# A streaming encoder on one NeuronCore: the merging gates of the first 768 tokens computed as paired products in the projection phase

## The chip, the cores and the metric

The kernel runs on 1 core of one Trainium2 chip. The metric is the device time of one execution in microseconds (us); lower is better. A NeuronCore has a matrix engine (TensorE, PE in the profile, with its weight loads shown as PEld), three engines for elementwise work (VectorE = DVE, ScalarE = ACT, GpSimd = POOL), and SyncE (SP), whose queue issues the DMA transfers here. The engines run side by side, each in its own program order, and wait for each other by semaphores.

## What is computed

One layer with two attention branches. T is 2048 prompt tokens and 128 new tokens of eight running streams, 2176 in all; the model width is 1024. Cut to what matters:

```python
h = rms_norm(x, g_in)
proj = einsum('btd,de->bte', h, w_in)
qa, ka, va, z_a, qd, ckv_in, kpe_in, z_b, m_a, m_b = split(proj)
o_a = diff_attention(...)            # 4 heads, two softmaxes each
o_b = mla_attention(...)             # 4 heads on a compressed latent
y_a = einsum('btw,wd->btd', rms_norm(o_a) * silu(z_a), w_oa)
y_b = einsum('btw,wd->btd', o_b * silu(z_b), w_ob)
merged = sigmoid(m_a) * y_a + sigmoid(m_b) * y_b     # m_a, m_b: the merging gates
out = x + einsum('btd,de->bte', merged, w_out)
```

The merging gates m_a and m_b are 2 x 1024 columns of the input projection: 16 units of 128 columns. The kernel stores tanh(m/2) for each, in `c.smT`, and the last phase makes the sigmoid out of it. All of it is float32; a matmul of full accuracy is made of three float32r matmuls (high x high, low x high, high x low parts of the operands).

## The kernel before

Work runs in five phases, one after the other on the whole: A, the input projections; A2, the second projections of the latent branch (Qn, Qp, Kn, Vb); B, the attention of the prompt; S, the attention of the streams; C, the output projections.

**Phase A** (`_phase_a`, L125) goes over three parts of the tokens (`PARTS`, L38: 768, 768 and 640 tokens, each cut in two halves of n = 384, 384 and 320 columns). A part first loads and normalises its tokens, makes the V block and the rotary key block, and then runs 11 *pairs* (`pairs`, L396). A pair (`pair_products`, L326) computes two units of 128 output columns for both halves at once, by Strassen's scheme in Winograd's form: seven products of 12 matmuls each, 84 matmuls of n columns, where the plain form needs 96. Its weights (`pair_weights`, L292) are two loads of 512 KB, four sums on DVE (L304, kept for later parts by a store of 1 MB to `c.wsum`, L305) and seven splits into high and low parts (`_split`, ACT L114 and DVE L115); its outputs are put together by one ACT copy and seven DVE additions (L335). The weight tiles have eleven buffers in two pools, so they are made ahead of the matmuls.

**The merging gates** are not in phase A. `_gates` (L423) computes them for one group of tokens (`GROUPS`, L36: five groups of 384 and a sixth of 256), 16 units of 24 matmuls each into a single PSUM bank (pool `z_p`, tile `z`), followed by a tanh on ACT (L464) that frees the bank, and a store to `c.smT`. A unit's weights are either loaded as they are (512 KB) and split, or, with `ready`, loaded already split from the scratch `c.wz` (two loads of 512 KB); group 1 stores its split weights there (two stores of 512 KB a unit, L458). Weight tiles `zw` have four buffers, two units.

**What sets the order.** The kernel is written against a framework that orders each engine's instructions by a simulated timeline with priorities. Loads and evacuation of `_gates` get the priority of the point behind phase A (`ahead`), their matmuls that of the place where `_gates` is called, behind phase B. So the gate matmuls are *filler*: the scheduler places them on PE wherever its timeline has PE idle in A2 and B. The order that it makes is fixed in the program; on the chip each engine keeps it. Groups 0, 1, 2 and 5 are called ahead of `_sample` (L1377) and fill A2 and B; groups 3 and 4 fill phase S. In the order of before, A2 holds the 384 matmuls of group 0, and phase B the 1152 of groups 1, 2 and 5.

**Phase B** (`_phase_b`, L1006) runs 4 heads x 8 blocks of 256 queries, 32 steps, each a block of the differential branch (its blocks upwards) and one of the latent branch (downwards): scores on PE, row maximum on DVE (L1077), exponential on ACT (L1079), scaling on POOL and DVE, transposes on PE, splits on ACT and DVE, products with the values on PE.

Of the kernel before, what the change touches and what calls it, by code (L numbers as in the profile page):

```python
# [14 lines left out]
AF = mybir.ActivationFunctionType  # L15
# [24 lines left out]
PARTS = [(0, 384), (768, 384), (1536, 320)]  # L40
# [72 lines left out]
def _split(nc, hi, lo, src):  # L113
    nc.scalar.copy(hi, src)  # L114
    nc.vector.tensor_tensor(lo, src, hi.bitcast(F32), op=ALU.subtract)  # L115
# [13 lines left out]
def _phase_a(c):  # L129

    nc, tc = c.nc, c.tc
    with (
# [14 lines left out]
        def stage(shape, name):  # L147
            return turn("st", 2, pst, c.zs).tile(shape, F32, tag="st", name=name)

        def operand(shape, name):  # L150
            return turn("w", 3, pw, c.zw).tile(shape, F32R, tag="w", name=name)
# [140 lines left out]
        def pair_weights(p, u, nm):  # L292
            st = [stage([P, KT, P], f"ws_{nm}_{i}") for i in range(2)]
            nc.sync.dma_start(st[0], c.i["wu"][u])
            sums = pq.tile([P, 4, 4, P], F32, tag="s", name=f"s_{nm}")
            a11, a12 = (st[0][:, k : k + 4] for k in (0, 4))
            s1, s2, s3, s4 = (sums[:, i] for i in range(4))
            if p == 0:
                nc.sync.dma_start(st[1], c.i["wu"][u + 1])
                a21, a22 = (st[1][:, k : k + 4] for k in (0, 4))  # L300
                for out, x, y, op in (
                    (s1, a21, a22, ALU.add), (s2, s1, a11, ALU.subtract), (s4, a12, s2, ALU.subtract), (s3, a11, a21, ALU.subtract)
                ):
                    nc.vector.tensor_tensor(out, x, y, op=op)  # L304
                nc.sync.dma_start(c.wsum[u // 2], sums)  # L305
            else:

                a22 = st[1][:, 4:8]
                nc.sync.dma_start(sums, c.wsum[u // 2])
                nc.sync.dma_start(a22, c.i["wu"][u + 1][:, 4:8])  # L310
            ops = []
            for i, x in enumerate((a11, a12, s4, a22, s2, s3, s1)):
                w = operand([P, KT, P], f"w{i}_{nm}")
                _split(nc, w[:, 0:4], w[:, 4:8], x)
                ops.append(w)
            return ops
# [37 lines left out]
        def rope_pair(p, u, dst, pair, out, scale):  # L354
            t0, n = PARTS[p]
            res = pair_products(p, u, f"r{u}_{p}")
            for half in range(2):
                nm = f"r{u}_{p}_{half}"
                cols = slice(t0 + half * n, t0 + half * n + n)
                cs = pc.tile([P, 2, NG], F32, tag="cs", name=f"cs{nm}", bufs=2)[:, :, :n]  # L360
                nc.sync.dma_start(cs, c.i["rope"][:, :, cols])
                co, si = cs[:, 0], cs[:, 1]
                ta, tb = res[0][half], res[1][half]
                m1, m2, m3, m4 = (tmp(n, f"m{i}{nm}") for i in range(4))
                nc.vector.tensor_tensor(m1, ta, co, op=ALU.mult)
                nc.vector.tensor_tensor(m2, tb, si, op=ALU.mult)
                nc.vector.tensor_tensor(m3, tb, co, op=ALU.mult)
                nc.vector.tensor_tensor(m4, ta, si, op=ALU.mult)
                nc.vector.tensor_tensor(m1, m1, m2, op=ALU.subtract)
                nc.vector.tensor_tensor(m3, m3, m4, op=ALU.add)  # L370
                for a, (r, x, y) in enumerate(((m1, ta, m2), (m3, tb, m4))):
                    if out is not None:
                        nc.sync.dma_start(out[pair, a, :, cols], r)
                    xr, yr = x.bitcast(F32R), y.bitcast(F32R)
                    nc.scalar.mul(xr, r, scale)
                    nc.vector.scalar_tensor_tensor(yr, r, scale, x, op0=ALU.mult, op1=ALU.subtract)
                    for hl, z in enumerate((x, y)):
                        nc.sync.dma_start(dst[pair, hl, a, :, cols], z)
# [8 lines left out]
        def gate_pair(p, u, out):  # L387
            t0, n = PARTS[p]
            res = pair_products(p, u, f"g{u}_{p}")
            for i in range(2):  # L390
                for half in range(2):
                    z = res[i][half]
                    nc.scalar.activation(z, z, AF.Silu)
                    nc.sync.dma_start(out[i][:, t0 + half * n : t0 + half * n + n], z)

        def pairs(p):  # L396
            rope = [lambda a=a: rope_pair(p, 2 * a, c.Qs, a, None, DIFF_SCALE) for a in range(2)]
            rope += [lambda a=a: rope_pair(p, 4 + 2 * a, c.Ks, a, c.o["kT"], 1.0) for a in range(2)]
            lat = [lambda a=a: latent_pair(p, 8 + 2 * a, [c.qdT[2 * a], c.qdT[2 * a + 1]]) for a in range(2)]
            lat.append(lambda: latent_pair(p, 12, [c.ckT[0], c.ckT[1]]))  # L400
            gate = [lambda a=a: gate_pair(p, 14 + 2 * a, [c.gzT[2 * a], c.gzT[2 * a + 1]]) for a in range(4)]
            mixed = [f for z in zip(rope, gate) for f in z]
            return [lat[0], *mixed, lat[1], lat[2]]

        for t in range(2 * PARTS[0][1] // P):
# [17 lines left out]
def _gates(c, prio, g, after, ready):  # L423

    nc, tc = c.nc, c.tc

    def ahead():
        return tc.high_priority(offset=tc.cur_priority - prio)

    t0, n = GROUPS[g]  # L430
    with ahead():
        R = c.zh.tile([P, NG], F32, tag="R", name=f"Rz{g}")[:, :n]
        nc.sync.dma_start(R, c.Rh[:, t0 : t0 + n])
        hi = c.zh.tile([P, KT, NG], F32R, tag="hi0", name=f"z_hi{g}")[:, :, :n]
        lo = c.zh.tile([P, KT, NG], F32R, tag="lo0", name=f"z_lo{g}")[:, :, :n]
        for k2 in range(4):
            x = c.zs.tile([P, 2, NG], F32, tag="st", name=f"zx{g}_{k2}")[:, :, :n]
            nc.sync.dma_start(x, c.i["xT"][:, 2 * k2 : 2 * k2 + 2, t0 : t0 + n])
            for j in range(2):
                k = 2 * k2 + j  # L440
                nc.vector.scalar_tensor_tensor(x[:, j], x[:, j], c.g_in[:, k : k + 1], R, op0=ALU.mult, op1=ALU.mult)
                nc.scalar.copy(hi[:, k], x[:, j])
                nc.vector.tensor_tensor(lo[:, k], x[:, j], hi[:, k].bitcast(F32), op=ALU.subtract)
    for u in range(16):
        nm = f"{g}_{u}"
        with ahead():
            w = [c.zw.tile([P, KT, P], F32R, tag="w", name=f"zw{l}_{nm}") for l in range(2)]
            if ready:
                for l in range(2):
                    nc.sync.dma_start(w[l].bitcast(F32), c.wz[u, l])  # L450
            else:
                st = c.zs.tile([P, KT, P], F32, tag="st", name=f"zs{nm}")
                nc.sync.dma_start(st, c.i["wu"][22 + u])
                for k in range(0, KT, 4):
                    _split(nc, w[0][:, k : k + 4], w[1][:, k : k + 4], st[:, k : k + 4])
                if g == 1:
                    for l in range(2):
                        nc.sync.dma_start(c.wz[u, l], w[l].bitcast(F32))  # L458
        ps = c.zp.tile([P, 512], F32, tag="z", name=f"z{nm}")[:, :n]
        with tc.issue_after(after) if after else nullcontext():  # L460
            _mm3(nc, ps, [(w[0][:, k], w[1][:, k], hi[:, k], lo[:, k]) for k in range(KT)])
        with ahead():
            s = c.zt.tile([P, NG], F32, tag="t", name=f"zt{nm}")[:, :n]
            nc.scalar.activation(s, ps, AF.Tanh, scale=0.5)  # L464
            nc.sync.dma_start(c.smT[u][:, t0 : t0 + n], s)
# [898 lines left out]
def build(tc, ins, outs, upto="z", dump=None):  # L1364
    c = Ctx()
    c.tc, c.nc = tc, tc.nc
    c.i, c.o = ins, outs
    with tc.tile_pool(name="const", bufs=1) as pool, tc.tile_pool(name="dram", bufs=1, space=DRAM) as dpool:
        _consts(c, pool)
        _scratch(c, dpool)  # L1370
        with ExitStack() as stack:
            _outer(c, stack)
            _phase_a(c)
            prio = tc.cur_priority
            _phase_a2(c)
            _phase_b(c)
            for g in (0, 1, 2, 5):  # L1377
                _gates(c, prio, g, None, g in (2, 5))
            _sample(c, stack)
            for g in (3, 4):  # L1380
                _gates(c, prio, g, c.mm.ins, False)
        _phase_c(c)
        for name, cut in (dump or {}).items():
            c.nc.sync.dma_start(c.o["d_" + name], cut(getattr(c, name)))
# [92 lines left out]
```

## Time and profile before

| | us |
|---|---|
| median of 3 runs | 2594.69 (2593.53 to 2594.82) |
| the profiled execution | 2595.66 |
| its span, first to last instruction | 2593.9 |
| PE busy | 2418.1 (93%) |
| DVE busy | 1645.4 (63%) |
| ACT busy | 1224.7 (47%) |
| POOL busy | 470.4 (18%) |
| DMA queue 1 moved | 550.46 MB, 64.0% of the time of 16 engines |

The shares are averages over phases with different limits, so they are to be read by phase: A ends at 621 us (its last pair matmul), A2 at 874 us, phase B at 1778, S at 2187. "PE busy" counts matmuls from start to modelled end, and matmuls overlap; the number of matmuls in a stretch is the firmer measure. PEclk is the share of full TensorE clock that was granted. "DMA" is the mean busy share of the core's 16 DMA engines.

### The profile page before, as it was taken

What the parts mean: (1) busy time and instruction counts of PE and PEld (TensorE: products, weight loads), DVE (VectorE), ACT (ScalarE), POOL (GpSimd) and SP (SyncE); (2) the same over time, 40 slices, a digit from 0 to 9 for tenths busy, and PEclk for the clock granted to TensorE, in tenths of its full rate; (3) what the DMA queues carried; (4) which work ended last, traced back from release to release, by engine and by line L of the source; (5) the groups of instructions that cost most, each with busy time, mean ns of one, the idle gap of its engine ahead of it and who ended that gap; (6) DMA issues with size and microseconds to landing.
All of it is one profiled execution on the core that took longest, in us unless ns stands there. A gap on an engine that the chain in (4) does not pass through costs nothing. (4 is left out here: it accounts for less than half of the span.)

```text
span 2593.9 us, 44001 instructions
## 1 busy us (share of the span) xinstructions
PE 2418.1 (93%) x15426; PEld 2149.4 (83%) x15426; DVE 1645.4 (63%) x3668; ACT 1224.7 (47%) x3042; POOL 470.4 (18%) x730
## 2 busy tenths in 40 slices
PE   6998999997899699999999988998999997999998
PEld 5998999997888689899888977887676674988887
DVE  7897686886676477877776688894333223534334
ACT  5544544543444366766665566783334333311111
POOL 0000000000000032333343234443000002122211
PEclk9999999999899899999999999999999998999999
DMA  6977677686687986574666755316869594544332
GB/s 236 306 268 251 210 252 265 204 280 185 228 277 255 299 285 201 183 227 140 182 194 207 232 170 166 92 58 232 325 254 370 222 380 138 174 128 126 121 115 96
DMA packets 303997, 553.28 MB, mean 213 GB/s; under 512 B 29184, under 2 KB 230176, under 8 KB 288544
## 3 DMA queue, kind: packets, MB, share of 16 engines
q1 hardware_dynamic: 303776, 550.46, 64.0%
q8 instruction: 123, 2.02, 0.3%
q14 instruction: 98, 0.80, 0.1%
HBM read 397.16 MB, written 153.19 MB: 212 GB/s over the span
## 5 line engine op out<-in xcount | busy, mean ns | idle before, releaser
L100 PE MATMUL z<-z_hi,zw 128*128 128x384 f32 (+1 forms) x768 | 264.7, 345 | 47.1 <-ACT zt L464 28.2
L102 PE MATMUL z<-z_hi,zw 128*128 128x384 f32 (+1 forms) x768 | 257.9, 336 | 0.4 <-DVE zw L115 0.4
L101 PE MATMUL z<-z_lo,zw 128*128 128x384 f32 (+1 forms) x768 | 258.1, 336 | 0.1
L1079 ACT ACTIVATE ed<-sd,pmd 128x512 f32<-128x512 f32 (+3 forms) x320 | 201.1, 632 | 43.6 <-DVE pmd L1077 23.0
L1077 DVE TENSOR_REDUCE pmd<-sd 128x1 f32<-128x512 f32 (+3 forms) x320 | 189.4, 603 | 49.9 <-PE sd L1178 30.6
L1178 PE MATMUL sd<-k,q 128*128 128x512 f32 (+2 forms) x640 | 193.1, 391 | 13.3 <-ACT ed L1079 8.9
L100 PEld LDWEIGHTS z<-z_hi,zw 128*128 128x128 f32 x768 | 148.6, 193 | 68.6 <-ACT zt L464 36.1
L1118 POOL TENSOR_SCALAR ed<-ed,ad 128x512 f32<-128x512 f32 (+3 forms) x160 | 115.5, 737 | 317.5 <-DVE ad L1094 142.5
L101 PEld LDWEIGHTS z<-z_lo,zw 128*128 128x128 f32 x768 | 148.8, 194 | 7.3 <-issue 4.1
L102 PEld LDWEIGHTS z<-z_hi,zw 128*128 128x128 f32 x768 | 147.9, 193 | 6.5 <-issue 3.4
L109 POOL TENSOR_SCALAR ss<-ss 128x3 f32<-128x3 f32 (+3 forms) x15 | 3.2, 213 | 792.4 <-DVE ss L529 474.1
L115 DVE TENSOR_TENSOR zw<-zs,zw 128x512 fp32r<-128x512 f32 x128 | 84.4, 688 | 92.9 <-ACT zw L114 90.8
L100 PE MATMUL y<-o,wh_ab 128*128 128x384 f32 (+1 forms) x384 | 127.8, 333 | 13.7 <-DVE sm L1303 10.5
L1118 POOL TENSOR_SCALAR em<-em,am 128x512 f32<-128x512 f32 (+3 forms) x160 | 102.9, 660 | 185.5 <-DVE am L1094 115.5
L101 PE MATMUL y<-o,wh_ab 128*128 128x384 f32 (+1 forms) x384 | 126.6, 330 | 0.0
L102 PE MATMUL y<-o,wl_ab 128*128 128x384 f32 (+1 forms) x384 | 126.3, 329 | 0.0
L1178 PEld LDWEIGHTS sd<-k,q 128*128 128x128 f32 x640 | 105.4, 194 | 23.6 <-ACT ed L1079 15.5
L1079 ACT ACTIVATE em<-sm,pmm 128x512 f32<-128x512 f32 (+3 forms) x160 | 100.2, 629 | 47.0 <-DVE pmm L1077 34.2
L1303 DVE SCALAR_TENSOR_TENSOR sm<-sm,y 128x384 f32<-128x384 f32 (+1 forms) x96 | 50.4, 530 | 112.9 <-PE y L102 111.4
L1308 ACT ACTIVATE m<-sm 128x384 fp32r<-128x384 f32 (+1 forms) x48 | 24.3, 506 | 199.0 <-POOL sm L1306 199.0
L1077 DVE TENSOR_REDUCE pmm<-sm 128x1 f32<-128x512 f32 (+3 forms) x160 | 95.6, 603 | 35.3 <-PE sm L1225 27.4
L1135 ACT CAST pthd<-ptd 128x512 fp32r<-128x512 f32 (+3 forms) x160 | 82.6, 522 | 72.1 <-PE ptd L1132 69.6
(521 smaller groups left out, 7579.3 us busy)
## 6 DMA issues: line engine op xcount, KB each, us to landing
zs<-in_wu_dram SPq DMA_DIRECT2D x64, 512.0 KB
zw<-wz SPq DMA_DIRECT2D x64, 512.0 KB
ksd<-in_ckT_dram SPq DMA_DIRECT2D x32, 1024.0 KB
vsd<-in_cv_dram SPq DMA_DIRECT2D x32, 1024.0 KB
q<-Qs SPq DMA_DIRECT2D x128, 128.0 KB
wz<-zw SPq DMA_DIRECT2D x32, 512.0 KB
ksm<-in_cc_dram SPq DMA_DIRECT2D x16, 1024.0 KB
smT<-zt SPq DMA_DIRECT2D x80, 192.0 KB
```

Source lines behind the costliest of these rows:

```text
L100: nc.tensor.matmul(out, ah, bh, start=(j == 0), stop=False)
L101: nc.tensor.matmul(out, ah, bl, start=False, stop=False)
L102: last = nc.tensor.matmul(out, al, bh, start=False, stop=(j == n - 1))
L109: c.nc.gpsimd.tensor_scalar(ss, ss, scale, EPS, op0=ALU.mult, op1=ALU.add)
L115: nc.vector.tensor_tensor(lo, src, hi.bitcast(F32), op=ALU.subtract)
L1077: nc.vector.tensor_reduce(nm_, ps[:, :w], axis=AX.X, op=ALU.max, negate=True)
L1079: nc.scalar.activation(e[:, :w], ps[:, :w], AF.Exp, bias=nm_, accum_out=l[:, s, i : i + 1])
L1118: nc.gpsimd.tensor_scalar(p, p, a[:, 0, j : j + 1], 1.0, op0=ALU.mult, op1=ALU.mult)
L1135: nc.scalar.copy(hi, v)
L1178: nc.tensor.matmul(ps[:, :n], qs[s][:, j, qc], ks[s].tiles[i][:, :n], start=(j == 0), stop=(j == 1 and not last))
L1303: nc.vector.scalar_tensor_tensor(s, s, 1.0, ps, op0=ALU.add, op1=ALU.mult)
L1308: nc.scalar.mul(z[0], sm[0], 0.5)
```

## The change

The 16 units of merging gates of the first 768 tokens (groups 0 and 1) move into phase A: part 0 gets eight more pairs (`merge_pair`), behind the rotary and gate pairs and ahead of the last two latent pairs. Each is a pair like the others, with tanh on its four outputs and four stores of 192 KB to `c.smT`; its weight sums are not kept for later parts, since only part 0 uses them. `_gates` is then called for groups 2 and 5 alone ahead of `_sample`; group 2 splits its weights itself and stores them in `c.wz`, as group 1 did, and group 5 loads them from there. Groups 3 and 4 stay as they are.

```diff
+                if u < 22:
+                    nc.sync.dma_start(c.wsum[u // 2], sums)
...
+        def merge_pair(p, u):
+
+            t0, n = PARTS[p]
+            res = pair_products(p, 22 + u, f"m{u}_{p}")
+            for i in range(2):
+                for half in range(2):
+                    z = res[i][half]
+                    nc.scalar.activation(z, z, AF.Tanh, scale=0.5)
+                    nc.sync.dma_start(c.smT[u + i][:, t0 + half * n : t0 + half * n + n], z)
...
+            if p == 0:
+                mixed += [lambda u=u: merge_pair(p, u) for u in range(0, 16, 2)]
             return [lat[0], *mixed, lat[1], lat[2]]
...
-                if g == 1:
+                if g == 2:
                     for l in range(2):
                         nc.sync.dma_start(c.wz[u, l], w[l].bitcast(F32))
...
-            for g in (0, 1, 2, 5):
-                _gates(c, prio, g, None, g in (2, 5))
+            for g in (2, 5):
+                _gates(c, prio, g, None, g == 5)
```

In the order that the scheduler makes, three places differ most. In the rows below a name like `zw0_5_7` is the tile `zw`, high part (0), of group 5, unit 7; the last number of a name counts tiles.

In part 0 of phase A, the SP queue behind the last store of the silu gates (`gzT`). Before:

```order
L394 DMA gzT_86<-u3g20_0_2002 128x384
L309 DMA s_r0_1_2991<-wsum_96 128x2048
L385 DMA qdT_83<-m1l10_0_2142 128x384
L279 DMA ws_kpe1_2797<-in_wkpe_dram 128x512
L385 DMA qdT_83<-wl10_0_2145 128x384
```

Now:

```order
L395 DMA gzT_86<-u3g20_0_2002 128x384
L294 DMA ws_m8_0_0_2675<-in_wu_dram 128x1024
L405 DMA smT_87<-m1m0_0_2141 128x384
L299 DMA ws_m8_0_1_2676<-in_wu_dram 128x1024
L405 DMA smT_87<-wm0_0_2144 128x384
L405 DMA smT_87<-vm0_0_2142 128x384
L405 DMA smT_87<-u3m0_0_2143 128x384
```

The latent pairs and the loads of part 1 stand eight pairs later; per pair there are two weight loads and four stores.

In A2, the SP queue at the stores of Qn of the third group of tokens. Before:

```order
L601 DMA Qn_88<-qnz2_1_7369 128x2x384
L601 DMA Qn_88<-qnz2_2_7386 128x2x384
L560 DMA out_ckT_dram<-ck3_7313 128x2x384
L601 DMA Qn_88<-qnz2_3_7403 128x2x384
L509 DMA qd4_7593<-qdT_83 128x4x384
L610 DMA cs3_7764<-in_rope_dram 128x2x384
L511 DMA ck4_7595<-ckT_84 128x2x384
L583 DMA kcs4_7866<-in_ropek_dram 64x2x384
L465 DMA smT_87<-zt0_9_20027 128x384
L453 DMA zs0_13_20140<-in_wu_dram 128x1024
```

Now:

```order
L614 DMA Qn_88<-qnz2_1_8497 128x2x384
L623 DMA cs3_8892<-in_rope_dram 128x2x384
L463 DMA zw0_5_7_21666<-wz_95 128x1024
L463 DMA zw1_5_7_21667<-wz_95 128x1024
L478 DMA smT_87<-zt5_5_21631 128x256
L614 DMA Qn_88<-qnz2_2_8514 128x2x384
L463 DMA zw0_5_8_21698<-wz_95 128x1024
L463 DMA zw1_5_8_21699<-wz_95 128x1024
L614 DMA Qn_88<-qnz2_3_8531 128x2x384
L478 DMA smT_87<-zt5_6_21663 128x256
```

Where one load of a gate unit's weights stood, there are two units with two loads each. On PE all 384 matmuls of group 2 and all 384 of group 5 now stand inside A2; before, the 384 of group 0 did.

In the first steps of phase B, ACT, whose tanh (`zt`) frees the gates' PSUM bank; `em`, `ed` are exponentials. Before:

```order
L1079 ACTIVATE em0_7_0_0_0_8528,lm0_7_0_8516<-sm0_7_0_0_0_8521,pmm0_7_0_8515 128x512
L1189 ACTIVATE sqd0_0_8453<-od0_0_8446 128x256
L114 CAST shd0_0_8457<-sqd0_0_8453 128x256
L464 ACTIVATE zt1_2_20393<-z1_2_20368 128x384
L1198 COPY sqd0_0_8453<-od0_0_8446 1x256
L1079 ACTIVATE em0_7_0_1_0_8537,lm0_7_0_8516<-sm0_7_0_1_0_8530,pmm0_7_0_8515 128x512
L464 ACTIVATE zt1_3_20431<-z1_3_20406 128x384
L1079 ACTIVATE em0_7_0_2_0_8546,lm0_7_0_8516<-sm0_7_0_2_0_8539,pmm0_7_0_8515 128x512
```

Now:

```order
L1092 ACTIVATE em0_7_0_0_0_9656,lm0_7_0_9644<-sm0_7_0_0_0_9649,pmm0_7_0_9643 128x512
L1202 ACTIVATE sqd0_0_9581<-od0_0_9574 128x256
L1092 ACTIVATE em0_7_0_1_0_9665,lm0_7_0_9644<-sm0_7_0_1_0_9658,pmm0_7_0_9643 128x512
L114 CAST shd0_0_9585<-sqd0_0_9581 128x256
L1211 COPY sqd0_0_9581<-od0_0_9574 1x256
L1092 ACTIVATE em0_7_0_2_0_9674,lm0_7_0_9644<-sm0_7_0_2_0_9667,pmm0_7_0_9643 128x512
```

No gate unit is left in phase B: neither its matmuls on PE, nor its tanh on ACT, nor its loads and stores.

## Rows read from the trace of the kernel before

**Rows 1.** Busy time in phases A, A2, B with filler, B without filler.

```profile
core 0: us, PE busy (x) PEld busy (x) DVE busy (x) ACT busy (x) POOL busy (x), PEclk, DMA share, GB/s
0.00:621.00 621.00, 582.94 (x3310) 560.99 (x3310) 489.92 (x971) 299.95 (x601) 5.83 (x18) 0.99 0.74 245
621.00:874.00 253.00, 209.20 (x1151) 201.13 (x1152) 169.95 (x351) 113.10 (x226) 13.87 (x28) 0.92 0.80 252
874.00:1535.00 661.00, 640.07 (x4272) 582.81 (x4272) 478.87 (x1231) 414.06 (x1168) 220.10 (x358) 0.98 0.66 209
1535.00:1778.00 243.00, 217.63 (x1414) 183.24 (x1413) 208.49 (x546) 173.97 (x506) 101.96 (x155) 0.95 0.37 107
```

**Rows 2.** The same stretches, instructions on the gates' bank `z` alone.

```profile
621.00:874.00 253.00, 82.45 (x384) 75.18 (x384) 7.77 (x16) 0.92 0.80 252
874.00:1535.00 661.00, 222.45 (x1152) 185.72 (x1152) 21.55 (x47) 0.98 0.66 209
1535.00:1778.00 243.00, 0.26 (x2) 0.44 (x2) 0.39 (x1) 0.95 0.37 107
```

**Rows 3.** Busy time: the 11 pairs of part 0; six pairs of part 1.

```profile
69.70:239.70 170.00, 165.51 (x937) 164.39 (x936) 139.23 (x264) 75.91 (x144) 1.54 (x2) 0.98 0.83 278
301.40:388.76 87.36, 87.36 (x506) 87.36 (x506) 70.01 (x135) 40.01 (x73) 1.37 (x2) 1.00 0.71 233
```

**Rows 4.** Groups of DVE and ACT in 0 to 250 us: busy us, mean ns.

```profile
L115 DVE TENSOR_TENSOR w_g<-ws_g,w_g 128x512 fp32r<-128x512 f32 x12 | 8.2, 680 | 0.1
L304 DVE TENSOR_TENSOR s_g<-s_g,ws_g 128x512 f32<-128x512 f32 x4 | 2.7, 680 | 0.0
L335 DVE TENSOR_TENSOR vg<-p3g,vg 128x384 f32<-128x384 f32 x4 | 2.2, 545 | 0.0
...
L114 ACT CAST w_g<-ws_g 128x512 fp32r<-128x512 f32 x12 | 7.4, 618 | 5.5 <-PE p4g L324 1.5 <-PE p6g L324 1.5 <-PE p3g L324 1.4
L393 ACT ACTIVATE m1g<-m1g 128x384 f32<-128x384 f32 x4 | 2.1, 524 | 4.3 <-DVE m1g L335 4.3
L338 ACT COPY m1g<-p1g 128x384 f32<-128x384 f32 x4 | 1.9, 472 | 0.0
```

**Rows 5.** DMA issues of the page: count in the whole program, size of one.

```profile
zs<-in_wu_dram SPq DMA_DIRECT2D x64, 512.0 KB
zw<-wz SPq DMA_DIRECT2D x64, 512.0 KB
...
wz<-zw SPq DMA_DIRECT2D x32, 512.0 KB
smT<-zt SPq DMA_DIRECT2D x80, 192.0 KB
```

**Rows 6.** Short stretches: inside A2, its end, the start of B, phase S.

```profile
720.00:740.00 20.00, 20.00 (x116) 19.26 (x114) 15.35 (x30) 8.59 (x18) 0.00 (x0) 1.00 0.89 292
...
860.00:880.00 20.00, 3.21 (x17) 2.79 (x15) 8.73 (x21) 7.55 (x18) 1.58 (x4) 0.62 0.78 239
880.00:900.00 20.00, 17.92 (x97) 17.02 (x98) 9.40 (x21) 9.29 (x25) 1.28 (x3) 0.86 1.04 357
...
1950.00:2000.00 50.00, 45.88 (x434) 33.29 (x427) 17.89 (x48) 20.30 (x56) 5.00 (x10) 1.00 1.00 395
```

**Rows 7.** Waits of PE from 621 to 890 us: total, times, longest.

```profile
PE z L100 <- ACT zt L464: 19.3, 8, 4.5
PE z L100 <- ACT zw L114: 18.3, 2, 10.9
PE lam_ps L666 <- DVE lam_pr L664: 11.2, 1, 11.2
```

**Rows 8.** Phase B without filler: the head change, late steps, the last head.

```profile
1555.00:1575.00 20.00, 14.21 (x72) 11.21 (x73) 17.99 (x43) 14.71 (x41) 9.74 (x12) 0.67 0.39 111
1675.00:1695.00 20.00, 19.33 (x135) 16.66 (x134) 19.03 (x54) 16.04 (x48) 9.23 (x15) 1.00 0.29 85
...
1606.80:1778.00 171.20, 160.56 (x1066) 137.20 (x1065) 145.71 (x395) 124.40 (x362) 74.50 (x116) 0.97 0.26 76
```

More of the change, by code (lines that the diff above doesn't have):

```diff
@@ L304, in pair_weights @@
                     nc.vector.tensor_tensor(out, x, y, op=op)
-                nc.sync.dma_start(c.wsum[u // 2], sums)
+                if u < 22:
+                    nc.sync.dma_start(c.wsum[u // 2], sums)
             else:
```

## The prediction

> **What bounds the kernel now.** I read the busy time by phase first [rows 1]. The span's 93% PE says little by itself, since only the phases that the change touches matter, and they are bound by different things. Phase A is matmul-bound: 583 of 621 us PE, and in part 1 six pairs follow each other with PE at 87.36 of 87.36 us [rows 3]. In phase A2 PE is busy for 209.2 of 253 us while the DMA engines are busy to 0.80 of theirs [rows 1]; PE waits there mostly for the gates' own filler: 19.3 us for the tanh that frees the one bank, 18.3 us for split weights, and 11.2 us at the end before the first work of B [rows 7]. In phase B up to 1535 us, where filler runs, PE is busy for 640 of 661 us. From 1535 to 1778 us the filler is used up (2 of its matmuls fall there [rows 2]), PE does 218 of 243 us, and DVE is at 208 of 243 [rows 1], 19.03 of 20 in late steps [rows 8]. So the trace already holds a piece of phase B as the change leaves all of it: without filler. That piece carries the largest term.
>
> **The change, part by part.** *Matmuls.* Two groups of 16 units at 24 matmuls go, 768; eight pairs at 84 come, 672. A pair of 384 columns takes 87.36 / 6 = 14.56 us, 173.3 ns a matmul [rows 3]. On PE alone the change is worth 96 x 173.3 ns = 16.6 us. Whether any of it is seen depends on where the time was, and that changes by phase.
>
> *Phase A, added.* Eight pairs at 14.56 us are 116.5 us, all on the path, since PE has next to no gap there. Does another engine stretch them? A new pair costs DVE seven splits at 0.680 us, four sums at 0.680 and seven additions at 0.545, 11.3 us; ACT seven splits at 0.618, a copy at 0.472 and four tanh, priced as the silu of the gate pairs at 0.524, 6.9 us [rows 4]. Both lie below 14.56 and beside it. Transfers are two loads of 512 KB and four stores of 192 KB, 1.84 MB in 14.56 us or 126 GB/s, where part 0 moved 278 [rows 3]. Without that cover the bound is part 0 itself: its 11 pairs took 170.0 us, 15.45 each [rows 3], but these include the rotary pairs, with far more DVE work, and the norm factors of the next part. So 116.5 us, up to 123.6. In SP's queue the latent stores and the loads of part 1 come eight pairs later, together with the matmuls that they wait for or feed, which costs nothing further.
>
> *Phase A2, changed.* Group 0's 384 matmuls are replaced by those of groups 2 and 5: the order puts all 768 into A2. Seen from PE: group 2 stands for group 0; group 5 has 256 columns, so its 384 matmuls add 384 x 173.3 ns x 256/384 = 44.4 us, or, taken from the 82.45 us that group 0 was busy [rows 2], 55 us. That makes 254 to 264 us of PE work. PE was idle for 253 - 209.2 = 43.8 us; of these 22.1 lie at the two ends (10.9 for the first weights, 11.2 at the end [rows 7]), where nothing can fill them. So 276 to 286 us if the rest of the idle time is filled, 298 to 308 if none is. Seen from the DMA engines: A2 moved 253 us x 252 GB/s = 63.8 MB in 0.80 x 253 = 202 us of all 16 engines. Added are group 2's 32 stores to `wz` and group 5's 32 loads from it, 512 KB each [rows 5], 16.8 MB each way; 16 stores of group 5's tanh (128 KB each), its tokens, and the first four weight units of group 3, which now stand at the end of A2: 38.8 MB in all. At A2's 252/0.80 = 315 GB/s they take 123 us, at the 395 GB/s that phase S reached [rows 6] 98 us. The sum is 300 to 325, less some 11 us of loads for B that ended in these 253 us (0.78 of 14 us [rows 6]): 289 to 314 us if the engines stay full throughout, as they did at 880 us [rows 6]. Both views meet near 300. I take 303, +50 us, since neither resource will be free of gaps; ends 276 (+23) and 325 (+72).
>
> For this term there is a price on a page too. The Trainium skill (DMA: Bandwidth & Descriptors, Bandwidth) gives 425 GB/s for transfers of 16 MB; by that all 102.6 MB would take 241 us and the transfers would hide behind PE, an estimate from that page and the second rival below. The rows show 315 in A2 itself, 395 at most.
>
> *Phase B, relieved.* It loses 1152 matmuls, their tanh, group 1's splits and some 59 MB of weight transfers; nothing is added. What remains is 4272 + 1414 - 1152 - 2 = 4532 matmuls [rows 1, 2]. Without filler PE got through 1412 of them in 243 us, 5.81 a us: 780 us for all. In the last head alone, 1066 in 171.2 us [rows 8], 6.23 a us: 728 us. To both come some 14 us at the start, where PE did 3.21 of 20 us [rows 6], waiting for B's first keys. That bounds phase B by 742 and 794 us. I take 775, near the long stretch: it holds a change of head, where PE did 14.2 of 20 us at a granted clock of 0.67 with DVE at 18.0 [rows 8], and three of four heads end in one. I go below its end because the drain at 1778 comes once only. That is 904 - 775 = -129 us, between -162 and -110. In other words, filler that takes 1152 matmuls out of B frees less than the 178 us that they take at full rate (768 x 173.3 ns and 44.4), since part of it ran in gaps that DVE leaves.
>
> Taken by PE's busy time, the term is another: B's own 640.07 + 217.63 - 222.71 = 635 us, at the 0.895 of the stretch without filler, are 710, with the start 724: -180 us. I don't take it, because overlapping matmuls of the filler count too much in the 222.71 (193 ns a matmul, of which a third have 256 columns, against 173.3 for a full one). The Trainium skill says the same from its side (Perfetto Trace Analysis, Identifying the Most-Contended Engine): busy time of matmuls is no good measure of headroom, that of weight loads is. By weight loads, (582.81 + 183.24 - 186.16) / 0.754 + 14 = 783 us, the trace agrees with the count.
>
> *Phases S and C* keep their instructions. Group 3's first loads stand earlier, ahead of B, where they delay it by the few us counted above.
>
> *Sum.* 116.5 + 50 - 129 = +37.5 us. The profiled execution took 2595.66, so 2633.2; it lies 0.97 above the median of the runs shown, so 2632.
>
> **The rivals.** *Faster: phase B gains what busy time says.* If steps without filler run as in the last head throughout, B takes 742 us (-162), and with the middle of A2's idle time filled (286, +33) the sum is 116.5 + 33 - 162 = -12.5: 2582. For it speaks that PE reaches 19.33 of 20 us in late steps without filler [rows 8]. Against it: DVE, at 19.03 there, has no slack to catch up after a head change. It decides at B = 737 us with A2 as forecast, at 754 with A2 at 286.
>
> *The transfers of A2 hide.* Then A2 ends at PE's 276 us (+23) and the sum is 116.5 + 23 - 129 = +10.5: 2605. For it: A2's engines had a fifth of their time left, and weight rows are long. Against it: in the middle of A2 the share was already 0.89 at 292 GB/s [rows 6].
>
> *A2 stalls unit by unit.* A unit of group 5 can be loaded only when the unit two before it is through, and SP issues in order: a load stands behind stores that wait for DVE, a store of Qn behind loads that wait for PE. If the 16 further units wait as group 0's did (19.3 + 18.3 - 10.9 = 26.7 us [rows 7]) and the old idle time stays, A2 takes 264 + 43.8 + 26.7 = 335 us (+82): 116.5 + 82 - 129 = +69.5, 2664.
>
> *The change does only what it says:* 96 matmuls fewer, the filler moved without loss. Then -16.6 us, 2578. It needs every idle slot of B to be worth nothing, which the 25 us that PE idles in 243 without filler, against 21 in 661 with it [rows 1], contradict.
>
> **How the numbers follow.** The forecast has 0.50, the stall 0.17, the hidden transfers 0.13, the faster B 0.15, the lossless move 0.05. The ends of the terms give 116.5 + 23 - 162 = -22.5 (2572) and 123.6 + 72 - 110 = +85.6 (2680); cutting the far low corner, the range is 2578 to 2680, which holds all cases' middles. A measurement can tell 0.2% here, 5.2 us, so no change is 2589.5 to 2599.9. Faster has the two low cases, 0.20; no change 0.10, from the low edge of the hidden transfers and the forecast; slower 0.70.
>
> **What would show it.** Right: part 0 of phase A has 19 pairs, the eight new ones 14.6 us each with PE full, and A ends near 738 us; A2 takes about 300 us at a DMA share of 0.9 or more; B shows a PE share near 0.87, DVE near 0.85, and about 775 us. Wrong: new pairs well over 15 us apart (DVE or transfers bind them after all); A2 at 280 us or below (transfers hid); B under 745 us (filler there was dear, and the move pays).

## The result and the profile after

The changed kernel takes 2609.65 us (median of 4 runs, 2605.63 to 2613.39), the kernel before 2594.76 beside it (4 runs): a ratio of 1.0064, 95% interval 1.0050 to 1.0078. It is slower by 14.9 us; the forecast was slower by 37. The profiled execution took 2613.39 us (span 2611.6), the highest of the four, so phases are compared between the two profiled executions and the total between medians.

The first part of the page tells almost nothing: PE is busy for 2418.1 us in both kernels.

```profile
PE 2418.1 (93%) x15330; PEld 2129.0 (82%) x15330; DVE 1672.7 (64%) x3748; ACT 1233.7 (47%) x3058; POOL 468.2 (18%) x730
```

By phase there are three large differences that nearly cancel. Busy time of the changed kernel in phases A, A2 and B, then the last 243 us of B (the counterpart of the unfilled stretch in [rows 1]), the eight new pairs, and six pairs of part 1 as in [rows 3]:

```profile
core 0: us, PE busy (x) PEld busy (x) DVE busy (x) ACT busy (x) POOL busy (x), PEclk, DMA share, GB/s
0.00:736.30 736.30, 695.86 (x3982) 674.27 (x3982) 573.33 (x1116) 351.44 (x697) 6.35 (x18) 0.99 0.69 227
736.30:1036.30 300.00, 257.07 (x1535) 243.59 (x1535) 179.92 (x373) 125.69 (x254) 12.75 (x25) 0.96 0.97 341
1036.30:1797.60 761.30, 696.56 (x4532) 588.69 (x4533) 622.35 (x1689) 532.90 (x1564) 320.17 (x515) 0.96 0.41 119
1554.60:1797.60 243.00, 222.80 (x1448) 187.24 (x1448) 202.05 (x534) 173.63 (x507) 103.16 (x158) 0.96 0.33 94
208.99:325.60 116.61, 116.61 (x674) 116.61 (x674) 84.13 (x146) 53.09 (x97) 0.00 (x0) 1.00 0.50 162
...
417.90:505.26 87.36, 87.36 (x507) 87.24 (x507) 70.87 (x139) 39.98 (x74) 1.90 (x2) 1.00 0.74 243
```

| phase | before | after | difference | forecast |
|---|---|---|---|---|
| A | 620.9 | 736.3 | +115.4 | +116.5 |
| A2 | 252.9 | 300.0 | +47.1 | +50 |
| B | 904.2 | 761.3 | -142.9 | -129 |
| S | 408.2 | 403.8 | -4.4 | 0 |
| C | 407.7 | 410.2 | +2.5 | 0 |

The gates' bank alone, as in [rows 2]: all 768 matmuls of groups 2 and 5 are in A2, and B holds two stragglers (the first matmuls of group 3).

```profile
736.30:1036.30 300.00, 126.96 (x768) 118.31 (x768) 13.99 (x32) 0.96 0.97 341
1036.30:1797.60 761.30, 0.19 (x2) 0.31 (x3) 0.00 (x0) 0.96 0.41 119
```

What PE waits for in A2 after, beside [rows 7] (total us, times, longest): the wait for the tanh fell from 19.3 to 7.4 us although twice as many units pass the bank, and a little waiting for the stored split weights is new.

```profile
PE z L100 <- ACT zw L114: 9.9, 1, 9.9
PE lam_ps L679 <- DVE lam_pr L677: 8.8, 1, 8.8
PE z L100 <- ACT zt L477: 7.4, 14, 1.7
...
PE z L100 <- DMA zw<-wz: 2.1, 2, 1.5
```

### The profile page after: what moved, and what is told of

It is laid out like the page before. It is cut to its first block, busy times and chain, and to the rows that moved or that the text cites. A ratio compares the mean times of both kernels' runs of the same rounds, so it can differ in the third digit from the quotient of the medians.

```text
span 2611.6 us, 43918 instructions
## 1 busy us (share of the span) xinstructions
PE 2418.1 (93%) x15330; PEld 2129.0 (82%) x15330; DVE 1672.7 (64%) x3748; ACT 1233.7 (47%) x3058; POOL 468.2 (18%) x730
## 5 line engine op out<-in xcount | busy, mean ns | idle before, releaser
L100 PE MATMUL z<-z_hi,zw 128*128 128x384 f32 (+1 forms) x512 | 172.9, 338 | 28.9 <-ACT zt L477 16.8
L102 PE MATMUL z<-z_hi,zw 128*128 128x384 f32 (+1 forms) x512 | 167.4, 327 | 2.1 <-DMA zw<-wz 1.4
L101 PE MATMUL z<-z_lo,zw 128*128 128x384 f32 (+1 forms) x512 | 167.2, 327 | 0.0
L100 PEld LDWEIGHTS z<-z_hi,zw 128*128 128x128 f32 x512 | 97.6, 191 | 49.2 <-ACT zt L477 26.4
L115 DVE TENSOR_TENSOR zw<-zs,zw 128x512 fp32r<-128x512 f32 x96 | 63.1, 691 | 98.4 <-ACT zw L114 88.2
L1148 ACT CAST pthm<-ptm 128x512 fp32r<-128x512 f32 (+3 forms) x160 | 83.9, 525 | 73.1 <-PE ptm L1145 72.7
L1149 DVE TENSOR_TENSOR ptld<-ptd,pthd 128x512 fp32r<-128x512 f32 (+3 forms) x160 | 95.2, 601 | 28.4 <-ACT pthd L1148 27.9
```

The lines of the kernel that those rows point to most:

```text
L100: nc.tensor.matmul(out, ah, bh, start=(j == 0), stop=False)
L101: nc.tensor.matmul(out, ah, bl, start=False, stop=False)
L102: last = nc.tensor.matmul(out, al, bh, start=False, stop=(j == n - 1))
L1148: nc.scalar.copy(hi, v)
L1149: nc.vector.tensor_tensor(ptl[ch][:, :n, i * P : (i + 1) * P], v, hi.bitcast(F32), op=ALU.subtract)
```

## The experiments

Two questions were open. Why does the change lose, when it has 96 matmuls fewer? And why did B give back 143 us and not 129? Theory for the first: filler costs little where it stood before (holes of A2 and B), and a pair in phase A costs its full 14.56 us. Rivals: the stores and loads of split weights make A2 long, or the number of filler matmuls there does. A group of 384 columns has 384 x 173.3 ns = 66.5 us of issue time, group 5 with 256 columns 44.4 [rows 3]. All ratios below are to the kernel before, run beside each kernel. Phases are those of one profiled execution each. Phase A took 619.3 to 624.9 us in the four runs without pairs and 735.7 to 740.5 us in the six with eight, though none of these edits is in it, so a difference of less than some 5 us in a phase says little.

**Group 5 moved from A2 into B (changed kernel).**

```diff
+            if c.first_mm is None:
+                c.first_mm = c.mm.ins
             return o
...
+    c.first_mm = None
...
-            for g in (2, 5):
-                _gates(c, prio, g, None, g == 5)
+            _gates(c, prio, 2, None, False)
+            _gates(c, prio, 5, c.first_mm, True)
```

> The changed kernel with one edit: the matmuls of gate group 5 may stand only behind the first value product of phase B, so the 384 of them (256 columns, 44 us of issue) move from A2 into the first head of phase B; group 2 stays in A2. Changed kernel by phase: A 736, A2 300, B 761, S and C 814 us. Place theory (filler in A2 is paid in full, since transfers bind that phase; in B it costs 143 us for 178 us of issue time, 0.8 of it): A2 262 us at a DMA share below 0.97, B 761 + 0.8 x 44 = 796, in all some 3 us faster than the changed kernel. Rival 'matmuls are matmuls' (PE is the bound wherever filler stands): A2 -44, B +44, no difference. Rival 'only the DMA share of A2 counts': A2 down to 245 or so, B +36, 19 us faster.

Measured: 2614.12 us, 1.0071 (1.0055 to 1.0088), no different from the changed kernel. Phases A2 and B:

```profile
740.50:1003.70 263.20, 216.69 (x1151) 204.41 (x1150) 170.92 (x357) 112.88 (x226) 13.17 (x25) 0.90 0.90 313
1003.70:1802.10 798.40, 740.54 (x4916) 639.06 (x4917) 640.63 (x1705) 546.51 (x1592) 317.94 (x515) 0.96 0.47 138
```

A2 is 36.8 us shorter and B 37.1 us longer. Both phases came out as the place theory had priced them (262 and 796). In either place these 44.4 us of issue cost about 0.83 of themselves, so where group 5 goes doesn't matter.

**Both groups moved into B (changed kernel).** The same edit, with group 2 held back as well:

```diff
-            _gates(c, prio, 2, None, False)
+            _gates(c, prio, 2, c.first_mm, False)
             _gates(c, prio, 5, c.first_mm, True)
```

> The changed kernel with the matmuls of groups 2 and 5 both held back to phase B, so that A2 has no filler at all and B has 768 filler matmuls (111 us of issue). Place theory: A2 falls from 300 to about 180 us (before it had 253 with 78 us of filler), B rises from 761 by 0.8 x 111 = 89 to 850; in all 30 us faster than the changed kernel, which would be 15 us faster than the kernel before. Rival 'matmuls are matmuls': A2 -111 to 189, B +111 to 872, no difference to the changed kernel. Rival 'A2 is bound by its own chain of stores and loads, the filler there was free': A2 stays above 240 us, B +89, 30 us or more slower than the changed kernel.

Measured: 2639.61 us, 1.0172 (1.0152 to 1.0192). Phases A2 and B, and PE's largest wait in A2:

```profile
738.90:974.30 235.40, 155.47 (x768) 145.49 (x767) 145.93 (x309) 90.11 (x174) 12.80 (x25) 0.79 0.70 230
974.30:1821.70 847.40, 796.27 (x5299) 699.99 (x5300) 672.28 (x1753) 571.04 (x1644) 320.72 (x514) 0.97 0.54 164
```

```profile
PE pss L536 <- DVE sq L528: 53.4, 6, 16.9
```

The place theory fell: without any filler A2 still takes 235.4 us, not 180, and the whole is 28 us slower than the changed kernel by the ratios, which is the rival of A2's own chain (above 240 us, 30 slower) but for 5 us. PE is busy for 155 of these us and waits for DVE's squares. So group 2, 66.5 us of issue, costs 27.8 us there (235.4 to 263.2) and 49.0 us in B (798.4 to 847.4). The first group in A2 is the cheapest of the places priced here; filler in phase S was not priced.

**All four groups of the kernel before moved into B.**

The edits that set `c.first_mm` are those of the first experiment:

```diff
             for g in (0, 1, 2, 5):
-                _gates(c, prio, g, None, g in (2, 5))
+                _gates(c, prio, g, c.first_mm, g in (2, 5))
```

> The kernel before (no merge pairs), with one edit: the matmuls of its four filler groups 0, 1, 2 and 5 may stand only behind the first value product of phase B, so A2 has no filler and B has 1536 matmuls of it (245 us of issue), which now reach to the end of B. Place theory: A 621, A2 falls from 253 to about 180 us, B rises from 904 by 0.8 to 0.9 of group 0's 67 us, to about 961; in all 15 us faster than the kernel before. Rival 'matmuls are matmuls': A2 -73, B +67, 6 us faster at most. Rival 'B is full': B rises by more than 73 us, since PE is busy for 97% where filler stands already, and the kernel is slower than before.

Measured: 2631.19 us, 1.0133 (1.0115 to 1.0151). Phases A2 and B:

```profile
624.90:856.40 231.50, 151.76 (x766) 143.21 (x766) 146.42 (x309) 90.16 (x174) 12.68 (x25) 0.79 0.70 225
856.40:1813.10 956.70, 919.81 (x6067) 836.64 (x6068) 723.67 (x1817) 614.72 (x1724) 326.73 (x516) 0.98 0.60 184
```

The kernel was to be 15 us faster and is 35 us slower: A2 fell by 21.4 us in place of 73, while B rose by 52.5, near the 0.8 to 0.9 of 67 us that was expected. The price of filler in B is about the same at these four doses. Against 761.3 us without filler: 37.1 us for 44.4 of issue (one group), 86.1 for 110.9 (two), 142.9 for 177.4 (the kernel before), 195.4 for 243.9 (all four). That is 0.84, 0.78, 0.81 and 0.80. (The three runs below with other mixes and raw weights widen this to 0.69 to 0.91.)

**Raw weights: no stores and loads of split weights (changed kernel).** Groups 2 and 5 load the raw weights and split them themselves. The order then puts group 5's matmuls into B.

```diff
-                if g == 2:
+                if g == 9:
                     for l in range(2):
                         nc.sync.dma_start(c.wz[u, l], w[l].bitcast(F32))
...
-                _gates(c, prio, g, None, g == 5)
+                _gates(c, prio, g, None, False)
```

> The changed kernel without the scratch for split weights: groups 2 and 5 both load raw weights and split them, group 2 stores nothing. This takes 16.8 MB of stores out of A2 and 8.4 MB of loads out of group 5, and adds 32 splits on ACT and DVE (0.62 and 0.68 us each). By the order that the scheduler makes, group 2 stands in A2 and group 5 in the first head of B, as in the run that moves group 5 alone, so A2 of these two differs by the 16.8 MB of stores only. If transfers bind A2 there even with 384 matmuls, A2 is some 45 us shorter than in that run (16.8 MB at 341 GB/s is 49 us); if PE and the chain of group 0's kind bind it, it is within 10 us of that run and near the 253 us of the kernel before. In all: by transfers 40 us faster than the changed kernel, else within 10 us of the run that moves group 5.

Measured: 2596.92 us, 1.0001 (0.9987 to 1.0015), the changed kernel's loss undone. Phases A2 and B:

```profile
739.40:980.10 240.70, 207.37 (x1150) 199.60 (x1150) 165.36 (x345) 109.78 (x222) 14.29 (x25) 0.94 0.82 259
980.10:1781.70 801.60, 738.62 (x4915) 632.84 (x4916) 662.14 (x1749) 563.46 (x1628) 319.87 (x514) 0.97 0.45 131
```

Beside the first experiment, whose groups stand alike, A2 is 22.5 us shorter, with 259 GB/s in place of 313: between the 45 us that transfers alone were to give and the 10 of the other case. The first group then costs A2 5.3 us. In B, group 5 costs 801.6 - 761.3 = 40.3 us, 0.91 of its issue time. I took this for a sign that transfers alone make A2 long, and the next two runs were to show it.

**The same with both groups in A2 (changed kernel).** Raw weights, and the matmuls get the priority of their loads:

```diff
-                if g == 2:
+                if g == 9:
...
-        with tc.issue_after(after) if after else nullcontext():
+        with tc.issue_after(after) if after else ahead() if g in (2, 5) else nullcontext():
             _mm3(nc, ps, [(w[0][:, k], w[1][:, k], hi[:, k], lo[:, k]) for k in range(KT)])
...
-                _gates(c, prio, g, None, g == 5)
+                _gates(c, prio, g, None, False)
```

> The changed kernel with raw weights for groups 2 and 5 (no split weights are stored or read back) and all 768 matmuls of them placed in A2, as in the changed kernel. Theory (transfers of split weights are what stretches A2): A 738, A2 262 to 276 instead of 300, at a DMA share well under 0.97; B 761, together 2570 to 2587. Rival, that A2 is long because of the second group's matmuls, splits and waits: A2 290 to 300 and 2600 to 2613.

Measured: 2607.21 us, 1.0040 (1.0021 to 1.0060). Phases A2 and B:

```profile
736.60:1025.50 288.90, 254.25 (x1535) 245.77 (x1535) 191.92 (x393) 135.71 (x278) 13.48 (x25) 0.94 0.82 258
1025.50:1791.50 766.00, 698.91 (x4531) 590.15 (x4532) 630.83 (x1701) 538.30 (x1572) 319.77 (x515) 0.96 0.42 122
```

My theory fell: A2 takes 288.9 us at a DMA share of 0.82, not 262 to 276. The split weights account for the 11 us up to 300.0, of which 5 come back in B (766.0 against 761.3); the ratio's interval overlaps the changed kernel's. The other 48 us beside the run above come with the second group itself. PE idles for 80 of 235 us without filler, for 33 of 241 with one group and for 35 of 289 with two: the first group fills the holes that can be filled, and the second adds its time in full.

**Groups 0 and 5 in A2, 1 and 2 in B (kernel before).** No pairs, groups 0 and 5 with raw weights and with their loads' priority:

```diff
+        with tc.issue_after(after) if after else ahead() if g in (0, 5) else nullcontext():
...
-            for g in (0, 1, 2, 5):
-                _gates(c, prio, g, None, g in (2, 5))
+            for g in (0, 5, 1, 2):
+                _gates(c, prio, g, None, g == 2)
```

> The kernel before with its four filler groups in another order and no pairs: groups 0 and 5, both with raw weights that are split on the spot, have all their matmuls placed in A2; groups 1 and 2 stay as filler of B. Theory (a place in A2 is cheap until transfers bind, and they bind only through the stores and loads of split weights; a place in B costs 0.80 of the issue time): A 621, A2 262 to 276 instead of 253 (PE is busy for 217 us with one group in A2, and group 5 adds 44 to 55), B 904 - 0.8 x 44 = 869, S and C unchanged, together about 2576 (2566 to 2590), faster than both kernels. Rival, that a second group in A2 always costs its 37 to 47 us, split weights or raw: A2 290 to 300, together about 2600.

Measured: 2603.47 us, 1.0029 (1.0014 to 1.0045). Phases A2 and B:

```profile
619.30:910.80 291.50, 256.79 (x1512) 247.96 (x1512) 189.68 (x387) 132.74 (x271) 15.32 (x28) 0.93 0.82 256
910.80:1787.60 876.80, 823.74 (x5324) 723.41 (x5324) 682.19 (x1771) 583.21 (x1658) 321.68 (x511) 0.98 0.54 165
```

The rival was right in a second kernel: A2 grows by 38.6 us, B shrinks by 27.4. (By the matmul counts, 24 of group 5's stayed in B. What B holds then costs 876.8 - 761.3 = 115.5 us for 135.8 of issue, 0.85.)

**Half of the change.** Four pairs for units 0 to 7; units 8 to 15 of groups 0 and 1 stay filler.

```diff
-                mixed += [lambda u=u: merge_pair(p, u) for u in range(0, 16, 2)]
+                mixed += [lambda u=u: merge_pair(p, u) for u in range(0, 8, 2)]
...
-    for u in range(16):
+    for u in range(8 if g in (0, 1) else 0, 16):
+        ready = g == 5 or g in (1, 2) and u > 7
...
-                if g == 2:
+                if g == (0 if u > 7 else 2):
...
-            for g in (2, 5):
-                _gates(c, prio, g, None, g == 5)
+            for g in (0, 1, 2, 5):
+                _gates(c, prio, g, None, False)
```

> Half of the change: four merging pairs (units 0 to 7) in place of eight; units 8 to 15 of the first 768 tokens stay filler, with groups 2 and 5 whole. 625 filler matmuls stand in A2 and 455 in B. Prices as the runs so far show them: A 621 + 4 x 14.5 = 679; A2 241 with 384 matmuls and 289 to 300 with 768, so 271 to 282 here; B 761 + 0.8 x 61 = 810; S and C 814; together 2574 to 2585, below both kernels. Rival, that the gain and loss are linear in the number of pairs: 2602, midway between the two kernels.

Measured: 2598.91 us, 1.0008 (0.9994 to 1.0021). Phases A, A2 and B:

```profile
0.00:678.90 678.90, 638.41 (x3646) 616.64 (x3646) 531.00 (x1044) 326.78 (x649) 7.77 (x18) 0.98 0.72 235
678.90:976.80 297.90, 262.95 (x1439) 250.28 (x1440) 180.59 (x373) 122.50 (x244) 14.73 (x28) 0.94 0.97 330
976.80:1780.30 803.50, 751.24 (x5012) 647.46 (x5011) 647.56 (x1721) 552.00 (x1605) 318.09 (x512) 0.98 0.50 147
```

A (679) came out as priced, B (810 expected) 6.5 us below; A2 did not: 297.9 us where 271 to 282 were expected. The gates' bank alone in A2:

```profile
678.90:976.80 297.90, 134.64 (x672) 122.14 (x672) 13.20 (x27) 0.94 0.97 330
```

The expectation had 625 filler matmuls in A2 and 455 in B; the run has 672 and, without a straggler of group 3, 480. It also counted matmuls and not their columns: all 672 have 384 columns, 672 x 173.3 ns = 116.5 us of issue, a little more than the 110.9 us of the changed kernel's 768, half of which have 256. At the same DMA share of 0.97, A2 costs what it costs there (300.0). B's 480 are 61.0 us of issue for 803.5 - 761.3 = 42.2 us, 0.69. The total is no different from the kernel before: the gain did not come, and it lies just below midway between the kernels, too.

**Group 3's preparation put back into B (changed kernel).** This one and the next are on B. In the kernel before, group 3's tokens are prepared at about 1545 us, right where the stretch began from which the prediction took B's rate; in the changed kernel this happens at the end of A2. Here half of it, with the splits of two units, is held back to the same place:

The place is a mark set in B, in lines not shown:

```diff
...
+                with tc.issue_after(c.marks['d2_5']) if g == 3 and k > 3 else nullcontext():
                     nc.vector.scalar_tensor_tensor(x[:, j], x[:, j], c.g_in[:, k : k + 1], R, op0=ALU.mult, op1=ALU.mult)
```

> The changed kernel with the second half of group 3's token preparation, and with it the splits of its first two weight units, held back from the end of A2 to the first step of B's last third, where the kernel before had them. Theory (the stretch from which B was extrapolated was slow by this one-off work on VectorE): the last 243 us of B, now 1448 matmuls, go back towards the 1414 of before, so B grows by 3 to 6 us; A2 loses the loads, 2 to 5 us; together within 4 us of the changed kernel. Rival, that the stretch of before was slow for the filler's last transfers or for the clock: B unchanged within 1.5 us.

Measured: 2605.37 us, 1.0037 (1.0019 to 1.0056). Phases A2 and B, and the last 243 us of B:

```profile
735.70:1031.80 296.10, 255.75 (x1534) 242.77 (x1534) 173.52 (x361) 121.34 (x246) 12.85 (x25) 0.96 0.97 338
1031.80:1789.70 757.90, 692.00 (x4531) 583.67 (x4532) 628.39 (x1702) 537.61 (x1572) 321.26 (x516) 0.97 0.43 123
1546.70:1789.70 243.00, 220.76 (x1429) 185.19 (x1428) 205.14 (x543) 175.62 (x510) 104.25 (x159) 0.96 0.37 104
```

A2 is 3.9 us shorter as expected, but B did not grow; it is 3.4 us shorter. The last 243 us did go the way that was expected, from 1448 matmuls to 1429 (the kernel before: 1414), but the part of B ahead of them was faster. Over B as a whole the theory fell in this form: half of the preparation costs nothing net in a B that ran without filler up to there.

**Group 3's preparation taken away from there (kernel before).** All of it is held back to the middle of the last head.

```diff
...
+                with tc.issue_after(c.marks['d3_3']) if g == 3 else nullcontext():
                     nc.vector.scalar_tensor_tensor(x[:, j], x[:, j], c.g_in[:, k : k + 1], R, op0=ALU.mult, op1=ALU.mult)
```

> The kernel before with one thing moved: group 3's token preparation, and with it the splits of its first two weight units, leave the place near 1545 us, just after the filler has run out, for the middle of B's last head. Theory (the stretch from which the prediction extrapolated B was slow because this one-off work, some 10 us of VectorE, met the change of head there): the 32 us after 1535 hold 15 to 25 more matmuls than their 97, the marked work is over 3 to 6 us sooner, and as much is given back in the last head. Rival (VectorE is late there because the filler kept it and TensorE busy up to then, whatever is prepared): the 32 us still hold 90 to 105 matmuls. Both leave the whole within 4 us of the kernel before.

Measured: 2589.24 us, 0.9980 (0.9966 to 0.9995): faster than both kernels, by 5 us (1 to 9) where at most 4 were expected, for moving one-off work of which some ten us are DVE's. Busy time of the kernel before in the first 32 us of the unfilled stretch and in the rest of it, and then of this kernel:

```profile
1535.00:1567.50 32.50, 19.84 (x97) 13.79 (x95) 29.92 (x69) 22.85 (x66) 12.02 (x16) 0.80 0.57 173
1567.50:1778.00 210.50, 197.79 (x1320) 169.45 (x1320) 178.57 (x477) 151.12 (x441) 89.94 (x140) 0.97 0.34 96
```

```profile
1535.00:1567.50 32.50, 29.29 (x182) 22.56 (x180) 31.43 (x76) 26.32 (x78) 16.45 (x23) 1.00 0.49 142
1567.50:1773.50 206.00, 187.86 (x1231) 158.37 (x1231) 176.51 (x473) 146.81 (x426) 84.42 (x130) 0.97 0.36 104
```

182 matmuls in place of 97, more than the 15 to 25 extra that I expected, and 1.00 in place of 0.80 for the clock. The rival (90 to 105) fell. The same work, up to one value product in the last third of B and from it to the end of B, in the kernel before (the second row is above), in this kernel, and in the changed kernel from there on:

```profile
1500.50:1567.50 67.00, 54.34 (x362) 46.39 (x361) 53.72 (x125) 43.97 (x121) 26.88 (x39) 0.90 0.54 164
```

```profile
1500.10:1554.30 54.20, 51.07 (x359) 44.25 (x357) 42.63 (x106) 36.28 (x103) 24.71 (x39) 1.00 0.48 145
1554.30:1773.50 219.20, 200.98 (x1323) 169.60 (x1323) 189.49 (x501) 158.43 (x459) 90.99 (x138) 0.97 0.37 106
```

```profile
1584.10:1797.60 213.50, 199.79 (x1325) 169.94 (x1323) 179.47 (x481) 152.74 (x445) 89.74 (x139) 0.97 0.33 94
```

Of the 12.8 us won, 8.7 are given back where the preparation now stands (219.2 against 210.5). DVE is about as busy in both stretches of 32 us, so what stands in its queue there matters, not how full it is. Its groups in the 32 us, in the kernel before (busy us, mean ns):

```profile
L1077 DVE TENSOR_REDUCE pmd<-sd 128x1 f32<-128x512 f32 (+3 forms) x18 | 10.5, 599 | 0.6 <-PE sd L1178 0.6
...
L443 DVE TENSOR_TENSOR z_lo<-zx,z_hi 128x384 fp32r<-128x384 f32 x8 | 4.2, 545 | 0.0
L441 DVE SCALAR_TENSOR_TENSOR zx<-zx,vec,Rz 128x384 f32<-128x384 f32 x4 | 2.9, 761 | 0.0
...
L115 DVE TENSOR_TENSOR zw<-zs,zw 128x512 fp32r<-128x512 f32 x4 | 2.7, 680 | 0.6 <-ACT zw L114 0.6
```

9.8 us are group 3's (4.2 + 2.9 + 2.7), and the row maxima of the differential branch's scores, on which PE depends, come 18 times, against 26 with the preparation moved. DVE's work is not all that moved, though. ACT's casts of the same preparation and the loads of its weights went with it, and waits of these 32 us show them:

```profile
PE ptd L1132 <- DVE ed L1125: 4.0, 1, 4.0
PE sd L1178 <- ACT em L1079: 3.6, 1, 3.6
ACT zw L114 <- DMA zs<-in_wu_dram: 2.3, 1, 2.3
```

PE's two longest waits are one for DVE and one for an exponential on ACT, which stands in ACT's queue behind the cast of group 3's first weights, and that cast waits 2.3 us for their load. So the run shows that the preparation as a whole makes the stretch slow; which part of it does is open. B as a whole goes from 904.2 to 897.3 us.

## Why the prediction was right and wrong

**Right: phase A.** Forecast +116.5, measured +115.4. The new pairs follow each other 14.56 us apart, PE is busy for 116.61 of 116.61 us, and DVE and ACT lie beside it (84 and 53 us), as priced from [rows 4].

**Right: phase A2.** Forecast 303 us, measured 300.0, at a DMA share of 0.97. Both views, PE's and the transfers', had met near 300, and both are real: without the split weights A2 still takes 288.9. So PE's side alone lies above the 276 of the rival of hidden transfers, which is why that could not come true. The 425 GB/s at 16 MB of the Trainium skill (DMA: Bandwidth & Descriptors, Bandwidth) were not reached: A2 sustained 341 GB/s with its engines at 0.97.

**Wrong: phase B, the term taken at 775 us.** It took 761.3, inside its ends of 742 and 794, but 14 us from the value that I took "near the long stretch". The failed step is the reading of 1535 to 1778 us as a sample of B without filler. Of its 243 us the first 32 hold 97 matmuls, because group 3's preparation stood there; what follows runs at 1320 / 210.5 = 6.27 a us, and the changed kernel takes 213.5 us from the same value product to the end of B (1325 matmuls). I had the 17.99 of 20 us of DVE and the clock of 0.67 before me in [rows 8], and read them as a change of head that comes three times, not as one event. Scaled up by 4532 / 1414, it was counted 3.2 times. The last 243 us of B hold 1429 to 1472 matmuls in the eight other runs whose filler is used up by then, none as few as 1414, and the fewest in the one with half of the preparation there; but the spread among these eight, 43, is no smaller than the step from 1414 to 1448. With the preparation moved, the same stretch holds 182 + 1231 = 1413 matmuls in 238.5 us, which for 4532 is 765 us; the choice I made then (14 us for the start, and 19 below that end) gives 760. That choice held by luck: in the changed kernel the last 243 us run at 1448 / 243 = 5.96 matmuls a us and B as a whole, its start included, at 4532 / 761.3 = 5.95, so nothing had to be added for the start, and the 19 us that I took off for another reason covered it. The run that put half of the preparation into the changed kernel's B took 19 matmuls out of its last 243 us and made B no longer, so the ten us of work are not a price by themselves. That they cost so much in the kernel before because DVE was already late when the filler ran out is argued, not shown, and so is the share of the late weight load; whether the other half of the preparation would have done it alone was not tried.

By weight loads I had 783 us for B, by matmul busy time 724. Against 761.3 the first was the nearer, 22 us off and not 37: weight loads were busy for 588.69 us in the end, where 579.89 had been worked out, and PE for 697, where 635 had. The Trainium skill (Perfetto Trace Analysis, Identifying the Most-Contended Engine) warns against busy time of matmuls and names that of weight loads; this trace agrees.

**The size of the sum.** +115.4 + 47.1 - 142.9 - 4.4 + 2.5 = +17.7 between the profiled executions, +14.9 between medians. Of the 23 us between +37.5 and +14.9, B's term is 14, A and A2 together 4, S and C 2, and 3 come from the profiled execution that lies above its median. With three terms of 50 to 130 us, a miss of 11% in one was nearly as large as the whole result.

**The rivals.** A faster B (737 us or less) and hidden transfers (A2 at 276) did not come. The stall of unit by unit did not either: the tanh wait fell. (Its price was read a little high: the waits of [rows 7] run to 890 us, and of the 18.3 us for split weights only 10.9 lie in A2, so it was 19.3 us and not 26.7.) That the change keeps its 96 matmuls' worth of 16.6 us was the weakest, and the placing runs say why: taking groups 0 and 1 out frees 1157.1 - 1061.3 = 95.8 us of A2 and B, 0.72 of their 133 us of issue, while the eight pairs cost 115.4, 0.87 of it. Seven products in place of eight were bought where PE has no gap, to replace work that had been partly hidden. The order has its share in the loss: with raw weights and group 5 in B, the same pairs free 1157.1 - 1042.3 = 114.8 us of A2 and B and break even. The kernel before was not run with raw weights in its own order, so how much of that belongs to the pairs is open.

## What to carry to other kernels

Price filler by place before replacing it: here the first group in A2 cost 0.1 to 0.4 of its issue time, a second one 0.8 or more, and filler in B 0.7 to 0.9, so a saving of an eighth in matmuls, paid in a full phase, lost with this order and broke even at best. Count filler by columns, not by matmuls. Before a stretch is scaled up to a whole phase, split it and look for one-off work in it, and compare the same work in two runs, not the same length of time. Where a net of a few us comes from terms of 50 to 140, its size is known only as well as the largest term; here the sign was had and the size was not.

## What the runs showed of the hardware

The granted clock falls where PE waits, and its own work pays for it. In the kernel before, 4 us at a time from 1547 on, PE did 3.1, 1.4, 2.3, 0.9 and 3.1 us of work; the clock was 1.00 (2.4 GHz), 0.94 and then 0.50, the lower of its two levels (1.2 GHz). With the preparation moved it stayed at 1.00.

```profile
1547.00:1551.00 4.00, 3.09 (x15) 1.73 (x13) 4.00 (x10) 2.48 (x8) 0.07 (x1) 1.00 0.45 138
1551.00:1555.00 4.00, 1.36 (x8) 0.83 (x7) 3.36 (x8) 1.45 (x4) 0.00 (x0) 0.94 1.00 281
1555.00:1559.00 4.00, 2.25 (x5) 1.48 (x6) 3.42 (x10) 4.00 (x13) 0.00 (x0) 0.50 0.59 158
1559.00:1563.00 4.00, 0.86 (x3) 0.14 (x1) 3.44 (x10) 0.94 (x2) 1.16 (x2) 0.50 0.34 109
1563.00:1567.00 4.00, 3.10 (x12) 2.45 (x13) 3.56 (x5) 2.90 (x8) 4.00 (x6) 0.50 0.21 86
```

In A2 the same holds over a whole phase, and so filler partly pays for itself: without filler A2's own 768 matmuls kept PE busy for 155 us at a mean clock of 0.79, with 768 filler matmuls between them for 254.25 - 127.63 = 127 us at 0.94. The second number is the bank `z` alone in the run with raw weights and both groups in A2:

```profile
736.60:1025.50 288.90, 127.63 (x768) 122.03 (x768) 13.83 (x32) 0.94 0.82 258
```

Matmuls overlap, and the difference leaves all overlap to the filler, so 127 is a lower bound; weight loads of A2's own, taken the same way, fell from 145.49 to 245.77 - 122.03 = 123.74 us.
